# Eight experts streamed through one core: visiting them in an order worked out on chip

## The chip, the cores and the metric

The kernel runs on one core of a Trainium2 chip. The metric is the device time of one execution in microseconds (us). Before the change the median of three runs is 1410.58 us.

## The reference

Two decoder layers on 256 tokens of width 1024. Layer 0 has a convolution group beside an attention over a memory, then a dense SwiGLU. Layer 1 has a sliding-window attention beside the same memory attention, then the part that the change is about, eight experts of which each token uses two:

```
def moe_swiglu(h, router, we_gate, we_up, we_down):
    logits = (h @ router).astype(jnp.float32)
    top_v, top_i = lax.top_k(logits, TOP_K)
    top_w = jax.nn.softmax(top_v, axis=-1)
    gates = jnp.sum(jax.nn.one_hot(top_i, N_EXPERTS) * top_w[..., None], axis=-2)
    out = jnp.zeros_like(h)
    for e in range(N_EXPERTS):
        out = out + gates[..., e:e + 1] * swiglu(h, we_gate[e], we_up[e], we_down[e])
    return out
```

`swiglu(h, g, u, d)` is `(silu(h @ g) * (h @ u)) @ d`, with `g` and `u` 1024 x 3584 and `d` 3584 x 1024 for each expert, all float32. The sum over the experts may be taken in any order.

## The kernel before

After the two attention layers and the dense SwiGLU, the router's scores are worked out on chip, and for each token and expert its place among that expert's tokens (`posm`, L768) and its weight (`G`). With 256 tokens, two experts each and eight experts, an expert has 64 tokens on average. The kernel gives each expert a block of the first 64 tokens and a block of up to 32 more (`SL = 96`, L841); the second block is computed only if the expert has more than 64 tokens (`over`, L788). An expert with tokens past its 64th is called **long** here, one without **short**. (Tokens past the 96th would be done by a separate tail at the end; its branch is not taken here.)

**Rounds.** An expert's hidden width of 3584 is cut into four rounds of 896 (`rounds`, L681): 32 rounds, experts 0 to 7 in order. In a round, `gate_up` (L862) multiplies the gathered tokens `xe` with eight pieces of gate and up weights into the PSUM tiles `pa` and `pb` (L868). In the middle of it stand the transposes of the round before (`hidden_T`, L898) and, in some rounds, the scatter of a finished expert (L940) or the gather of the next one's tokens (L843). Then `over_parts` (L949) loads one flag into a register of TensorE's queue, and under `tc.If` (L956) does `gate_up_over` (L876, into `po`) for a long expert, and `down_over` (L927) for the round before, if that was of a long one. Last comes `down` (L917), which multiplies the hidden values of the round before with four pieces of down weights into `py`. The order on TensorE is written out by hand (L959); the other engines' order is the scheduler's.

**The weight stream.** Each round reads eight pieces of 896 KB (gate and up by turns) and four of the down matrix (three of 1024 KB, one of 512 KB). All are issued by SyncE's queue (SP) in the order of `units()` (L687 to L705): gate and up of round i, then down of round i-1. They go into a ring of 19 buffers of 1 MB (`RING`, L39): the piece number n waits until TensorE is done with the piece n-19. A gate or up piece is held until the round's `over_parts` is past, since both blocks read it. SP works in order, so a piece whose buffer is held also holds up all pieces behind it. `fetch` (L707, L991) writes the issues into the program a round at a time.

In the code after the change the same places stand some 50 to 60 lines further down.

Of the kernel before, what the change touches and what calls it, by code (L numbers as in the profile page):

```python
# [7 lines left out]
F32 = mybir.dt.float32  # L8
# [3 lines left out]
U32 = mybir.dt.uint32  # L12
AF = mybir.ActivationFunctionType
OP = mybir.AluOpType
AX = mybir.AxisListType
PSUM = bass.MemoryType.PSUM

P = 128
# [6 lines left out]
HD = 64  # L25
FF = 2816
NE = 8
# [20 lines left out]
def hybrid_kernel(  # L48
# [6 lines left out]
    nc = tc.nc  # L55
    act, dve, pool, pe, sp = nc.scalar, nc.vector, nc.gpsimd, nc.tensor, nc.sync
# [47 lines left out]
    for t in range(2):  # L104
# [5 lines left out]
                       channel_multiplier=1)  # L110
# [56 lines left out]
    with ExitStack() as ph:  # L167
# [377 lines left out]
        for i in range(NB):  # L545
# [15 lines left out]
            if prev is not None:  # L561
# [15 lines left out]
                           channel_multiplier=1)  # L577
        pool.affine_select(dist, dist, pattern=[[1, S]], compare_op=OP.is_ge, fill=BIG, base=-1,
                           channel_multiplier=-1)
# [11 lines left out]
        for blk in (2, 1, 0):  # L591
            w = [halves(load_rows(sw_w_in[0][i * 512:(i + 1) * 512, blk * 512:(blk + 1) * 512], 4),
                        after=last if blk == 1 else None) for i in range(2)]
# [29 lines left out]
        for n in range(2):  # L623
            for kp in range(2):
                b = bank("so", "so").rearrange("p (q n) -> p q n", n=P)
# [35 lines left out]
    with ExitStack() as ph:  # L661
        one = ph.enter_context(tc.tile_pool(name="one", bufs=1, reuse_waits="tile"))
# [14 lines left out]
        RW = 896  # L677
# [5 lines left out]
        def unit(v, src):  # L683
            sp.dma_start(v, src.rearrange("(k p) n -> p k n", p=P))  # L684
            return v

        def units():  # L687

            for i in range(len(rounds) + 1):
                if i < len(rounds):  # L690
                    e, p = rounds[i]
                    for q in range(4):
                        for w in (sw_we_gate, sw_we_up):
                            t = raw_tile()[:, :2 * RW].rearrange("p (k n) -> p k n", k=2)
                            yield unit(t, w[0, e, q * 256:(q + 1) * 256, p * RW:(p + 1) * RW])
                if i:
                    e, p = rounds[i - 1]
                    for q in range(4):
                        n = min(2, BLK - 2 * q)
                        t = raw_tile()[:, :n * D].rearrange("p (k n) -> p k n", k=n)  # L700
                        r0 = p * RW + 2 * q * P
                        yield unit(t, sw_we_down[0, e, r0:r0 + n * P, :])

        stream = units()
        ahead = []  # L705

# [10 lines left out]
        iota = one.tile([P, P], F32, name="iota")  # L717
        pool.iota(iota, pattern=[[1, P]], base=0, channel_multiplier=0, allow_small_or_imprecise_dtypes=True)

        rows2 = [one.tile([P, P], F32, name=f"rows2{n}") for n in range(2)]  # L720
        for n in range(2):
            o = (0, HD)[n]
            pool.tensor_copy(rows2[n][:, o:o + HD], iota[:, 0:HD])
            for q in range(2):
                pool.tensor_copy(rows2[n][:, HD - o + 32 * q:HD - o + 32 * q + 32], iota[:, HD:HD + 32])
        tri = one.tile([P, P], BF16, name="tri")
        pool.memset(tri, 1.0)
        pool.affine_select(tri, tri, pattern=[[1, P]], compare_op=OP.is_ge, fill=0.0, base=-1,
                           channel_multiplier=-1)
# [14 lines left out]
        for kk in range(KD // 2):  # L744
            b = prt.tile([P, 512], F32, name="rtb", tag="gu").rearrange("p (a n) -> p a n", a=2)
# [5 lines left out]
            for k in range(2 * kk, 2 * kk + 2):  # L751
                q = k % 4
# [15 lines left out]
        posm = one.tile([P, 2, NE], F32, name="posm")  # L768
# [12 lines left out]
        pn = bank("pn")  # L781
        for t in range(2):
# [3 lines left out]
                                 op0=OP.add, op1=OP.mult)  # L786
        dve.tensor_scalar_add(posm, posm, -1.0)
        over = one.tile([P, NE], I32, name="over")  # L788
        topi = one.tile([P, 1], I32, name="topi")
        G = one.tile([P, 2, NE], F32, name="G")  # L790
        dve.tensor_scalar(over, pn[:, :NE], float(HD), None, op0=OP.is_gt)
        top = one.tile([P, 1], F32, name="top")
        dve.reduce_max(top, pn[:, :NE], axis=AX.X)
        dve.tensor_copy(topi, top)
# [20 lines left out]
        def gates():  # L815

            gts = one.tile([P, 2, 2], F32, name="gts")
            dif = one.tile([P, 2, 1], F32, name="dif")
            eul = one.tile([P, 2], F32, name="eul")
            pool.memset(eul, 2.718281828459045)  # L820
            dve.tensor_tensor(dif, mx[:, :, 1:2], mx[:, :, 0:1], op=OP.subtract)
            ex = one.tile([P, 2], F32, name="ex")
            pool.tensor_tensor(ex, eul, dif[:, :, 0], op=OP.pow)
            den = one.tile([P, 2], F32, name="gden")
            dve.tensor_scalar_add(den, ex, 1.0)
            dve.reciprocal(gts[:, :, 0], den)
            dve.tensor_tensor(gts[:, :, 1], ex, gts[:, :, 0], op=OP.mult)
            for t in range(2):
                dve.tensor_scalar_mul(G[:, t, :], oh[:, t, 0, :], gts[:, t, 0:1])
                dve.scalar_tensor_tensor(G[:, t, :], oh[:, t, 1, :], gts[:, t, 1:2], G[:, t, :],  # L830
                                         op0=OP.mult, op1=OP.add)

        def places(e):

            Pm = [wk.tile([P, 2, P], F32, name=f"Pm{n}", tag=f"Pm{n}", bufs=1) for n in range(2)]
            for n in range(2):
                for t in range(2):
                    dve.tensor_scalar(Pm[n][:, t, :], rows2[n], posm[:, t, e:e + 1], None, op0=OP.is_equal)
            return Pm

        SL = 96  # L841
# [1 line left out]
        def gather(e, Pm):  # L843

            xe = wk.tile([P, KD, SL], F32, name="xe", tag="xe")
            for kk in range(2):
                b = bank("ga")[:, :4 * SL].rearrange("p (k n) -> p k n", k=4)
                for a in range(4):
                    k = kk * 4 + a
                    for t in range(2):  # L850
                        pe.matmul(b[:, a, :], hn[:, t, k * P:(k + 1) * P], Pm[0][:, t, :SL], start=(t == 0),
                                  stop=(t == 1))
                (act.copy if kk else dve.tensor_copy)(xe[:, kk * 4:kk * 4 + 4, :], b)
            b = bank("pmt")
            for n in range(2):
                for t in range(2):
                    pe.transpose(b[:, n * S + t * P:n * S + (t + 1) * P], Pm[n][:, t, :], ident)
            PT = wk.tile([P, 2, S], F32R, name="PT", tag="PT")
            act.copy(PT, b.rearrange("p (n s) -> p n s", n=2))
            return xe, PT  # L860
# [79 lines left out]
        def scatter(e, ys, PT):  # L940
            for n in range(2):
                for t in range(2):
                    b = bank("sc")
                    for i in range(2):
                        pe.matmul(b, PT[:, n, t * P:(t + 1) * P], ys[n][i], start=(i == 0), stop=(i == 1))
                    hs = h[:, t, n * 512:(n + 1) * 512]
                    dve.scalar_tensor_tensor(hs, b, G[:, t, e:e + 1], hs, op0=OP.mult, op1=OP.add)  # L947

        def over_parts(gu, dn):  # L949

# [7 lines left out]

        with tc.manual_schedule(engines={mybir.EngineType.PE}):  # L959
            xe = {0: gather(0, places(0))}  # L960
            gates()
            prev = None
            ys = None
            flag = None
            for i in range(len(rounds) + 1):
                last_round = i == len(rounds)
                if not last_round:
                    e, p = rounds[i]
                    wgu = [ahead.pop(0) for _ in range(8)]
                    if p == NR - 1 and e + 1 < NE:  # L970
                        Pm = places(e + 1)
                    gate_up(xe[e][0], wgu, range(4))
                if prev is not None:
                    wd = [ahead.pop(0) for _ in range(4)]
                    hT, hTo = hidden_T(*prev[2:])
                if ys is not None:
                    scatter(*ys)
                    ys = None
                if not last_round:
                    if p == NR - 1 and e + 1 < NE:  # L980
                        xe[e + 1] = gather(e + 1, Pm)
                    gate_up(xe[e][0], wgu, range(4, KD))
                    hx = hidden()
                over_parts(None if last_round else (e, p, xe[e][0], wgu), None if prev is None else (*prev[:2], hTo, wd))
                if prev is not None:
                    down(prev[1], hT, wd)
                    if prev[1] == NR - 1:
                        ys = (prev[0], outputs(), xe[prev[0]][1])
                if not last_round:
                    prev = (e, p, hx, hidden_over())  # L990
                    fetch(8 + 4 * (i > 0))  # L991
            scatter(*ys)
        finish()
        psm.close()
# [6 lines left out]
        def bank(name):  # L1001
# [6 lines left out]
                             skip_runtime_bounds_check_because="a count of 256 tokens")  # L1008
# [90 lines left out]
```

## Time and profile before

| | |
|---|---|
| median of 3 runs | 1410.58 us (1407.84 to 1410.89) |
| the profiled execution's own time | 1408.38 us |
| its span, first to last instruction | 1406.3 us |
| TensorE (PE) busy | 1290.9 us, 92% |
| VectorE (DVE) busy | 372.1 us, 26% |
| ScalarE (ACT) busy | 299.9 us, 21% |
| SP's DMA queue | 414.39 MB, 77.4% of 16 engines' span |
| mean granted clock of TensorE | 0.974 |

How to read it: a core's engines run side by side, each its own list of instructions in order, and wait for one another and for transfers. The shares are averages over the whole span; the experts' part is some 900 us of it, and has stretches with different limits. In the timelines PE is TensorE's matmul, an "x4" merges four like instructions, and square brackets give the idle time before an instruction and what ended it. "PEq" and "SPq" are the queues of TensorE and SyncE: instructions that load a register, branch or issue a transfer.

### The profile page before, as it was taken

What the parts mean: (1) busy time and instruction counts of PE and PEld (TensorE: products, weight loads), DVE (VectorE), ACT (ScalarE), POOL (GpSimd) and SP (SyncE); (2) the same over time, 40 slices, a digit from 0 to 9 for tenths busy, and PEclk for the clock granted to TensorE, in tenths of its full rate; (3) what the DMA queues carried; (4) which work ended last, traced back from release to release, by engine and by line L of the source; (5) the groups of instructions that cost most, each with busy time, mean ns of one, the idle gap of its engine ahead of it and who ended that gap; (6) DMA issues with size and microseconds to landing.
All of it is one profiled execution on the core that took longest, in us unless ns stands there. A gap on an engine that the chain in (4) does not pass through costs nothing. (4 is left out here: it accounts for less than half of the span.)

```text
span 1406.3 us, 18891 instructions
## 1 busy us (share of the span) xinstructions
PE 1290.9 (92%) x7908; PEld 711.0 (51%) x7908; DVE 372.1 (26%) x697; ACT 299.9 (21%) x575; POOL 70.2 (5%) x107
## 2 busy tenths in 40 slices
PE   6978899999889689999999999998888889999995
PEld 6844789999766533433344343443343343344342
DVE  5632554444676300102011111111111110100201
ACT  5423354444455010001001001111010010000100
POOL 5120100000030200000000000000000000000000
PEclk9989899999999899999999999999999999999998
DMA  9842155555470758899989989999999999999994
GB/s 294 290 120 57 61 197 190 183 180 180 111 244 1 288 198 312 316 361 367 377 335 378 360 334 361 405 406 406 407 406 407 407 407 406 407 407 406 404 407 189
DMA packets 149735, 420.90 MB, mean 299 GB/s; under 512 B 9658, under 2 KB 43256, under 8 KB 149624
## 3 DMA queue, kind: packets, MB, share of 16 engines
q1 hardware_dynamic: 145304, 414.39, 77.4%
q10 hardware_dynamic: 4320, 4.96, 1.1%
q8 instruction: 79, 1.29, 0.4%
q14 instruction: 32, 0.26, 0.1%
HBM read 417.37 MB, written 1.95 MB: 298 GB/s over the span
## 5 line engine op out<-in xcount | busy, mean ns | idle before, releaser
L868 PE MATMUL pa<-raw,xe 128*64 128x512 f32 x1024 | 302.9, 604 | 26.6 <-DMA raw<-in_sw_we_up_dram 19.1
L868 PE MATMUL pb<-raw,xe 128*64 128x384 f32 x1024 | 247.7, 493 | 0.0
L917 PE MATMUL py<-raw,hT 128*64 128x512 f32 x896 | 200.0, 596 | 17.2 <-PEq L956 16.0
L868 PEld LDWEIGHTS pb<-raw,xe 128*64 128x64 f32 x1024 | 87.8, 138 | 132.6 <-issue 128.7
L91 DVE TENSOR_TENSOR wlo<-raw,whi 128x1024 fp32r<-128x1024 f32 x108 | 131.9, 1260 | 81.7 <-ACT whi L90 81.7
L868 PEld LDWEIGHTS pa<-raw,xe 128*64 128x64 f32 x1024 | 83.3, 138 | 137.7 <-issue 86.7
L917 PEld LDWEIGHTS py<-raw,hT 128*64 128x64 f32 x896 | 66.6, 137 | 146.2 <-issue 114.0
L90 ACT CAST whi<-raw 128x1024 fp32r<-128x1024 f32 x112 | 111.5, 1046 | 55.5 <-issue 26.2
L876 PE MATMUL po<-raw,xe 128*32 128x512 f32 (+1 forms) x1024 | 113.1, 543 | 0.0
L910 DVE COPY hTo<-hto 128x224 f32<-128x224 f32 x32 | 12.5, 391 | 374.3 <-PE hto L908 374.3
L894 DVE TENSOR_TENSOR hxo<-so,po 64x384 f32<-64x384 f32 x32 | 17.8, 556 | 333.7 <-ACT so L893 333.7
L904 ACT COPY hT<-ht 128x448 f32<-128x448 f32 x32 | 17.0, 532 | 394.5 <-PE ht L902 394.5
L892 ACT ACTIVATE so<-po 64x384 f32<-64x384 f32 x32 | 15.4, 482 | 315.5 <-PE po L876 188.0
L876 PEld LDWEIGHTS po<-raw,xe 128*32 128x32 f32 x1024 | 39.6, 109 | 65.4 <-issue 59.2
L927 PE MATMUL py<-raw,hTo 128*32 128x512 f32 x448 | 65.5, 593 | 1.7 <-PEq L956 1.7
L98 PE MATMUL fg<-xh,whi 128*128 128x256 f32 x176 | 50.2, 285 | 2.7 <-ACT fsg L557 2.5
L98 PE MATMUL fu<-xh,whi 128*128 128x256 f32 x176 | 50.1, 284 | 0.0
L100 PE MATMUL fg<-xl,whi 128*128 128x256 f32 x176 | 50.0, 284 | 0.0
L99 PE MATMUL fu<-xh,wlo 128*128 128x256 f32 x176 | 50.0, 284 | 0.0
L99 PE MATMUL fg<-xh,wlo 128*128 128x256 f32 x176 | 50.0, 284 | 0.0
L100 PE MATMUL fu<-xl,whi 128*128 128x256 f32 x176 | 49.9, 284 | 0.0
L466 PE MATMUL pcv<-sh,bands 128*32 128x256 f32 x384 | 34.3, 425 | 12.1 <-DMA sh<-ud 12.0
(271 smaller groups left out, 1571.3 us busy)
## 6 DMA issues: line engine op xcount, KB each, us to landing
raw<-in_sw_we_gate_dram SPq DMA_DIRECT2D x128, 896.0 KB
raw<-in_sw_we_up_dram SPq DMA_DIRECT2D x128, 896.0 KB
raw<-in_sw_we_down_dram SPq DMA_DIRECT2D x96, 1024.0 KB
raw<-in_sw_we_down_dram SPq DMA_DIRECT2D x32, 512.0 KB
raw<-in_cv_w_gate_dram SPq DMA_DIRECT2D x11, 1024.0 KB
raw<-in_cv_w_up_dram SPq DMA_DIRECT2D x11, 1024.0 KB
raw<-in_cv_w_down_dram SPq DMA_DIRECT2D x11, 1024.0 KB
raw<-in_cv_w_in_dram SPq DMA_DIRECT2D x7, 1024.0 KB
```

What stands on the lines that cost most here:

```text
L90: act.copy(hi[:, i:i + step], v[:, i:i + step])
L91: (low or dve).tensor_tensor(lo[:, i:i + step], v[:, i:i + step], hi[:, i:i + step].bitcast(F32), op=OP.subtract)
L98: pe.matmul(ps, ah, bh, start=first, stop=False)
L99: pe.matmul(ps, al, bh, start=False, stop=False)
L100: pe.matmul(ps, ah, bl, start=False, stop=last)
L466: pe.matmul(pcv[q * 32:(q + 1) * 32, :], T[:, g, q, :], sh[q][:, 4 * g:4 * g + S], start=(g == 0), stop=(g == GT - 1), tile_position=(0, q ...
L868: pe.matmul(ps[half * HD:(half + 1) * HD, :c1 - c0], x, v[:, c0:c1], start=(k == 0), stop=(k == KD - 1), tile_position=(0, half * HD))
L876: pe.matmul(po[q * 32:(q + 1) * 32, :c1 - c0], x, v[:, k % 2, c0:c1], start=(k == 0), stop=(k == KD - 1), tile_position=(0, q * 32))
L894: dve.tensor_tensor(hx[:, :B], s[HD:, :B], po[HD:, :B], op=OP.mult)
L904: act.copy(hT, b[:, :3 * P + HD])
L917: pe.matmul(py[n][n * HD:(n + 1) * HD, :], hT[:, o:o + HD], w[q // 2][:, q % 2, n * 512:(n + 1) * 512], start=(p == 0 and q == 0), stop=(p ...
L927: pe.matmul(py[n][r:r + 32, :], hTo[:, o:o + 32], w[q // 2][:, q % 2, n * 512:(n + 1) * 512], start=(i < 2), stop=(i >= NR * BLK - 2), til ...
```

## The change

The experts are no longer taken in the order 0 to 7. Expert 0 stays first. For the others the order is worked out on VectorE from the eight counts: long and short ones by turns as far as both last, the first of them of the other kind than expert 0. The result is a row of eight indices `turn` and a 0/1 matrix `perm`, with which `posm`, `over` and `G` are put into the new order once (`posm2`, `over`, `G2`). The code of the rounds is then the same as before, with "expert e" meaning "the e-th in turn". The pieces of weights of all experts after the first are read from an address that depends on a register: SP loads `turn[e]` into a register once per expert, and each piece's address is that register times the size of one expert's matrix, plus a constant. Sizes, order and buffers of the pieces within an expert stay. The core of the diff:

```diff
+        turn = one.tile([P, NE], U32, name="turn")
+        whose = {0: 0}
+
+        def matrix(w, e):
+            if e not in whose:
+                whose[e] = nc.values_load(turn[0:1, e:e + 1], engines={mybir.EngineType.SP}, min_val=0, max_val=NE - 1,
+                                          skip_runtime_bounds_check_because="an index into eight numbers")
+            return w[0, 0] if e == 0 else w[0, bass.ds(whose[e], 1)][0]
...
-                            yield unit(t, w[0, e, q * 256:(q + 1) * 256, p * RW:(p + 1) * RW])
+                            yield unit(t, matrix(w, e)[q * 256:(q + 1) * 256, p * RW:(p + 1) * RW])
...
-                        yield unit(t, sw_we_down[0, e, r0:r0 + n * P, :])
+                        yield unit(t, matrix(sw_we_down, e)[r0:r0 + n * P, :])
...
+        before = one.tile([P, NE, NE], F32, name="before")
+        pool.memset(before, 1.0)
+        pool.affine_select(before, before, pattern=[[1, NE], [-1, NE]], compare_op=OP.is_ge, fill=0.0, base=-1,
+                           channel_multiplier=0)
+        pool.memset(before[:, :, 0:1], 0.0)
...
-        dve.tensor_scalar(over, pn[:, :NE], float(HD), None, op0=OP.is_gt)
+        dve.tensor_scalar(overf, pn[:, :NE], float(HD), None, op0=OP.is_gt)
...
+        def permuted(dst, src):
+            n = src.shape[1]
+            pr = one.tile([P, 2, NE, NE], F32, name="pr", tag="pr")
+            dve.tensor_tensor(pr[:, :n], perm[:, None].to_broadcast([P, n, NE, NE]),
+                              src[:, :, None, :].to_broadcast([P, n, NE, NE]), op=OP.mult)
+            dve.reduce_sum(dst, pr[:, :n], axis=AX.X)
+
+        def turns_of():
+            pr = one.tile([P, 2, NE, NE], F32, name="pr", tag="pr")[:, 0]
+            rk = one.tile([P, 4, NE], F32, name="rk")
+            val = one.tile([P, 8], F32, name="val")
+            turnf = one.tile([P, NE], F32, name="turnf")
+            dve.tensor_tensor(pr, before, overf[:, None, :].to_broadcast([P, NE, NE]), op=OP.mult)
+            dve.reduce_sum(rk[:, 0], pr, axis=AX.X)
+            dve.scalar_tensor_tensor(rk[:, 1], rk[:, 0], 2.0, iota[:, 0:NE], op0=OP.mult, op1=OP.subtract)
+            dve.scalar_tensor_tensor(rk[:, 2], rk[:, 1], 1.0, overf, op0=OP.add, op1=OP.mult)
+            dve.scalar_tensor_tensor(rk[:, 3], rk[:, 0], 1.0, iota[:, 0:NE], op0=OP.add, op1=OP.subtract)
+            dve.tensor_tensor(rk[:, 2], rk[:, 3], rk[:, 2], op=OP.subtract)
+            dve.tensor_scalar(rk[:, 1], overf, overf[:, 0:1], None, op0=OP.is_equal)
+            dve.scalar_tensor_tensor(val, rk[:, 2], 2.0, rk[:, 1], op0=OP.mult, op1=OP.subtract)
+            dve.memset(val[:, 0:1], 1.0)
+            best = one.tile([P, 8], F32, name="best")
+            dve.max(best, val)
+            dve.max_index(turn, best, val)
+            dve.tensor_copy(turnf, turn)
+            dve.tensor_tensor(perm, iota[:, None, 0:NE].to_broadcast([P, NE, NE]),
+                              turnf[:, :, None].to_broadcast([P, NE, NE]), op=OP.is_equal)
+            permuted(posm2, posm)
+            over2 = one.tile([P, 1, NE], F32, name="over2")
+            permuted(over2, overf[:, None, :])
+            dve.tensor_copy(over, over2[:, 0])
+
         def places(e):
+            pos = posm if e == 0 else posm2
...
-                    dve.tensor_scalar(Pm[n][:, t, :], rows2[n], posm[:, t, e:e + 1], None, op0=OP.is_equal)
+                    dve.tensor_scalar(Pm[n][:, t, :], rows2[n], pos[:, t, e:e + 1], None, op0=OP.is_equal)
...
-                    dve.scalar_tensor_tensor(hs, b, G[:, t, e:e + 1], hs, op0=OP.mult, op1=OP.add)
+                    dve.scalar_tensor_tensor(hs, b, G2[:, t, e:e + 1], hs, op0=OP.mult, op1=OP.add)
...
             xe = {0: gather(0, places(0))}
+            turns_of()
             gates()
+            permuted(G2, G)
```

On SP, at the place where the stream comes to the second expert (the last down pieces of the third round, then gate and up pieces of the fifth), there stood before:

```order
L684 DMA raw<-in_sw_we_down_dram 128x2x1024 x3
L684 DMA raw<-in_sw_we_down_dram 128x1024
L684 DMA raw<-in_sw_we_gate_dram 128x2x896
L684 DMA raw<-in_sw_we_up_dram 128x2x896
L684 DMA raw<-in_sw_we_gate_dram 128x2x896
```

and with the change, where ISA is an instruction that multiplies registers:

```order
L684 DMA raw<-in_sw_we_down_dram 128x2x1024 x3
L684 DMA raw<-in_sw_we_down_dram 128x1024
L693 TENSOR_LOAD turn
L684 ISA
L684 DMA raw<-in_sw_we_gate_dram 128x2x896
L684 ISA
L684 DMA raw<-in_sw_we_up_dram 128x2x896
L684 ISA
L684 DMA raw<-in_sw_we_gate_dram 128x2x896
```

One register load is added per expert after the first (7), and one ISA ahead of each of their pieces (7 x 48 = 336); no piece has moved in its queue.

On VectorE, at the start of the experts' part, between the gather matrix `Pm` of the first expert and the copy of its gathered tokens `xe`, there stood before:

```order
L838 TENSOR_SCALAR Pm_4455<-rows_4343,posm 128x128 x2
L827 TENSOR_TENSOR gts<-ex,gts 128x2
L829 TENSOR_SCALAR G<-oh,gts 128x8 x2
L830 SCALAR_TENSOR_TENSOR G<-oh,gts,G 128x8 x2
L853 COPY xe<-ga 128x384
```

and with the change:

```order
L895 TENSOR_SCALAR Pm_4464<-rows_4344,posm 128x128 x2
L869 TENSOR_REDUCE rk<-pr 128x8
...
L879 MAX best<-val 128x8
L880 MAX_INDEX turn<-best,val 128x8
L881 CAST turnf<-turn 128x8
L882 TENSOR_TENSOR perm<-iota,turnf 128x64
L858 TENSOR_TENSOR pr<-perm,posm 128x128
L860 TENSOR_REDUCE posm_4432<-pr 128x16
L910 COPY xe<-ga 128x384
L858 TENSOR_TENSOR pr<-perm,overf 128x64
```

Fourteen rows of the new ranking now stand ahead of that copy; one more (the product `pr` of `before` and `overf`, L868) stands ahead of `Pm`, and six behind the copy. On GpSimd (POOL) three rows that make `before` are added; on TensorE no instruction is added or moved.

## Rows read from the trace of the kernel before

**Rows 1.** DMA issues of the page: pieces of the weight stream, KB each.

```profile
raw<-in_sw_we_gate_dram SPq DMA_DIRECT2D x128, 896.0 KB
raw<-in_sw_we_up_dram SPq DMA_DIRECT2D x128, 896.0 KB
raw<-in_sw_we_down_dram SPq DMA_DIRECT2D x96, 1024.0 KB
raw<-in_sw_we_down_dram SPq DMA_DIRECT2D x32, 512.0 KB
```

**Rows 2.** Busy time by stretch: last three columns granted clock, DMA share, GB/s.

```profile
core 0: us, PE busy (x) PEld busy (x) DVE busy (x) ACT busy (x) POOL busy (x), PEclk, DMA share, GB/s
492.00:611.00 119.00, 115.29 (x747) 45.18 (x747) 11.49 (x28) 11.71 (x24) 0.00 (x0) 0.97 0.74 287
611.00:735.00 124.00, 124.00 (x814) 49.64 (x812) 15.01 (x31) 11.05 (x24) 0.00 (x0) 1.00 0.91 356
735.00:859.00 124.00, 124.00 (x814) 49.65 (x812) 15.01 (x31) 11.06 (x24) 0.00 (x0) 1.00 0.91 357
859.00:883.00 24.00, 23.11 (x130) 8.29 (x128) 2.39 (x5) 2.24 (x5) 0.00 (x0) 1.00 0.99 376
883.00:972.00 89.00, 84.42 (x446) 36.97 (x442) 15.02 (x31) 11.14 (x25) 0.00 (x0) 1.00 1.03 407
972.00:1083.00 111.00, 94.46 (x446) 41.76 (x446) 15.99 (x33) 12.05 (x26) 0.00 (x0) 0.98 1.03 407
1083.00:1197.00 114.00, 99.84 (x508) 44.11 (x509) 14.03 (x30) 9.98 (x22) 0.00 (x0) 0.99 1.03 407
1197.00:1316.00 119.00, 118.17 (x752) 47.14 (x750) 14.14 (x27) 11.06 (x24) 0.00 (x0) 1.00 1.03 406
```

**Rows 3.** The line of `gate_up_over`: in which of 40 slices it ran.

```profile
L876 PE MATMUL po<-raw,xe x1024: 486/552/617, 504.8 to 1282.0; 128*32 128x512 f32 x118, 128*32 128x384 f32 x53
busy tenths in 40 slices 0000000000000099999999999000000009999000
```

**Rows 4.** Timeline of TensorE: first matmuls of experts, `down_over` of expert 2, first missing piece.

```profile
611.25 1.03 PE L868 MATMUL pa<-raw,xe 128*64 128x512 f32 x4
735.20 1.03 PE L868 MATMUL pa<-raw,xe 128*64 128x512 f32 x4
859.13 1.03 PE L868 MATMUL pa<-raw,xe 128*64 128x512 f32 x4
873.42 3.63 PE L927 MATMUL py<-raw,hTo 128*32 128x512 f32 x28 [0.90 <-PEq L956]
951.03 1.06 PE L868 MATMUL pa<-raw,xe 128*64 128x512 f32 x4
972.52 1.04 PE L868 MATMUL pa<-raw,xe 128*64 128x512 f32 x2 [0.60 <-DMA raw<-in_sw_we_gate_dram]
1291.99 1.03 PE L868 MATMUL pa<-raw,xe 128*64 128x512 f32 x4
```

**Rows 5.** Waits of SP: which instruction waited for what, us in total, times, longest.

```profile
SPq L684 <- PE po L876: 253.2, 54, 32.5
```

**Rows 6.** Chain that ended last, two pieces: from a transfer's issue to its landing.

```profile
1351.67 16.97 DMA raw<-in_sw_we_gate_dram
1368.70 18.64 DMA raw<-in_sw_we_down_dram
```

**Rows 7.** Queue instructions: SP's issues, and register loads and branches of TensorE's queue.

```profile
459.58 0.37 SPq L684 DMA_DIRECT2D raw<-in_sw_we_up_dram  x1
460.04 0.42 SPq L684 DMA_DIRECT2D raw<-in_sw_we_gate_dram  x1
L954 PEldq TENSOR_LOAD <-over x64: 296/302/495, 501.1 to 1380.0; - x64
L956 PEldq COMPARE_BRANCH  x96: 65/169/431, 501.7 to 1380.4; - x96
```

**Rows 8.** Timeline of VectorE and TensorE at the start of the experts.

```profile
483.30 0.26 DVE L774 TENSOR_TENSOR oh<-iota,ixf 128x16 f32<-128x16 f32 x2
487.15 0.36 DVE L830 SCALAR_TENSOR_TENSOR G<-oh,gts,G 128x8 f32<-128x8 f32 x2
490.25 0.56 DVE L853 COPY xe<-ga 128x384 f32<-128x384 f32 x1 [2.74 <-PE ga L851]
492.64 1.08 PE L868 MATMUL pa<-raw,xe 128*64 128x512 f32 x4
```

More of the change, by code (lines that the diff above doesn't have):

```diff
@@ L788, in hybrid_kernel @@
         over = one.tile([P, NE], I32, name="over")
+        posm2 = one.tile([P, 2, NE], F32, name="posm2")
+        G2 = one.tile([P, 2, NE], F32, name="G2")
         topi = one.tile([P, 1], I32, name="topi")
         G = one.tile([P, 2, NE], F32, name="G")
-        dve.tensor_scalar(over, pn[:, :NE], float(HD), None, op0=OP.is_gt)
+        overf = one.tile([P, NE], F32, name="overf")
+        dve.tensor_scalar(overf, pn[:, :NE], float(HD), None, op0=OP.is_gt)
         top = one.tile([P, 1], F32, name="top")
@@ L831, in gates @@
                                          op0=OP.mult, op1=OP.add)
+        perm = one.tile([P, NE, NE], F32, name="perm")
+        def permuted(dst, src):
[28 more added lines that the diff above has]
+            dve.tensor_copy(over, over2[:, 0])
         def places(e):
+            pos = posm if e == 0 else posm2
             Pm = [wk.tile([P, 2, P], F32, name=f"Pm{n}", tag=f"Pm{n}", bufs=1) for n in range(2)]
```

## The prediction

> **What bounds the kernel now.** I read the stretches first, then TensorE's timeline, then the waits of SP and the chain that ended last.
>
> The weight stream is 128 + 128 pieces of 896 KB, 96 of 1024 KB and 32 of 512 KB [rows 1]: 352.3 MB, 44.04 MB an expert, 11.01 MB a round, and 0.918 MB a piece on average. The stretches [rows 2] show two regimes. From 883 us to 1316 us the transfers move 406 to 407 GB/s with little change, whatever TensorE does beside them: that is this stream's ceiling here, and at 407 GB/s an expert takes 108.2 us, a round 27.05 us and a piece 2.25 us. From 611 to 859 us they move only 356 and 357 GB/s, while TensorE is busy for all of the 248 us: there TensorE is the bound. Which experts these are is seen in the slices of the second block's matmuls [rows 3]: it runs in slices 14 to 24 and again in 33 to 36 (35.2 us each), so experts 0, 1, 2 and 6 are long, and 3, 4, 5 and 7 short.
>
> The timeline [rows 4] gives both prices on TensorE. A long expert after a long one takes 735.20 to 859.13, 123.9 us. The short one after it takes 859.13 to 951.03, 91.9 us, in which it still does the `down_over` of expert 2's last round, 3.63 us. So a long expert after a short one should take 123.9 - 3.6 = 120.3 us. The stream, at 108.2 us, lies between the two kinds: during a long expert it runs ahead until the ring is full, and then has to wait; during a short one TensorE eats up the lead.
>
> How large the lead can be shows after 859 us, where the ring is full. The four short rounds to 951.03 use up 108.2 - 91.9 = 16.3 us of it; the next round lasts to 972.52, 21.5 us against the stream's 27.05, 5.6 us more, and there TensorE waits for a piece for the first time [rows 4]. So a full ring is worth about **21.9 us** of lead.
>
> Three long experts in a row therefore cost what the ring cannot hold. SP waits 253 us in all for the second block to give buffers back, up to 32.5 us at a time [rows 5]. Afterwards three short ones in a row leave TensorE waiting for the stream. Both engines lose time, one after the other. The chain that ended last goes through two transfers of the stream near its end [rows 6]: the time of the whole is the stream's, plus what the stream lost before.
>
> **The change part by part.**
>
> *The order.* With these counts, the rank formulas give 0, 3, 1, 4, 2, 5, 6, 7: long and short by turns, a long one first and short expert 7 last, as before. The first long expert (to 611.25) and the change-over to a short one lose what they lose now. I then follow the lead from a full ring, 21.9 us: after expert 3, 5.6; expert 1 puts back 120.3 - 108.2 = 12.1, so 17.7; after 4, 1.4; after 2, 13.5; after 5, nothing, TensorE having waited 2.8; after 6, 12.1; at the end nothing, after another wait of 4.2. The lead never reaches 21.9 again, so the stream does not stop any more. What it loses now in experts 1 and 2 is saved: 124 x (1 - 356/407) + 124 x (1 - 357/407) = 15.5 + 15.2 = **30.8 us**. The 24 x (1 - 376/407) = 1.8 us of the change-over [rows 2] stay, as there is still one out of a full ring. That a long expert can run beside an unbroken stream is seen already: expert 6, after three short ones, has 406 GB/s from 1197 to 1316 us.
>
> *Whether TensorE is then the bound.* Its own path would be 611.25 + 3 x (91.9 + 120.3) = 1247.9 to the start of expert 7, and from there to the end of the span it takes 1406.3 - 1291.99 = 114.3 us today: 1362 us. The stream's end gives 1406.3 - 30.8 = 1375.5. The stream decides, by 13 us; this also limits a gain to 44 us.
>
> *Addresses from registers.* SP gets 336 register multiplications and 7 register loads. Before, no such multiplication is in the trace. The nearest rows [rows 7] are a branch on a register, 0.17 us, and a register load on TensorE's queue, 0.30 us; an issue takes 0.37 us and the next one comes 0.46 us later. With 0.30 us more each, twelve pieces of a round need 12 x 0.76 = 9.1 us of SP's 27. The last transfers on the chain take 17 and 18.6 us from issue to landing [rows 6], which is seven or eight pieces: SP is that far ahead, and a register load of 0.3 us, or a late multiplication, lies under this cover. I take nothing for it, between nothing (it can't speed up SP) and the price in the last rival. If a piece's address were needed while the ring is full, its buffer would be the later one anyway. SP reads `turn` only after three rounds of issues, long after VectorE made it; what stands behind that load are the pieces of the second expert, not needed for two more rounds.
>
> *The ranking.* One product is new ahead of `Pm` and so on TensorE's path: 0.13 to 0.26 us by its neighbours [rows 8], I take 0.2. Fourteen rows (15 instructions in a trace, since an index search shows as two) stand ahead of the copy of `xe`. At 0.18 to 0.26 us each [rows 8] they take 2.7 to 3.9 us. VectorE idles 2.74 us there, and the copy, which ends at 490.81, is wanted only when TensorE is through with its transposes at 492.64: 1.8 us more. The cover is 4.6 us, so nothing is lost; without it the sum would grow by up to 3.9 us. `over` is read 9 us later [rows 7], the second expert's `Pm` in the fourth round. GpSimd's three rows are on no chain.
>
> *The sum.* The profiled execution took 1408.38 us with a span of 1406.3, so 2.1 lie outside. 1408.4 - 30.8 + 0.2 = 1377.8 us. The median of the runs is 2.2 us above that execution: **1380.0 us**.
>
> **A rule that speaks against it.** The trace has the stream at 407 GB/s for over 400 us [rows 2]. The Trainium skill, DMA: Bandwidth & Descriptors, section Bandwidth, puts one core's share of its memory at about 358 GB/s and says that "For HBM↔SBUF transfers the HBM side (~358) binds". By that rule the 356 and 357 GB/s of experts 1 and 2 would already be the ceiling and nothing could be saved: 1410.6 us instead of 1380.0. The trace goes against it here; this core reads alone.
>
> **The rivals.**
>
> 1. *The ring fills up in other ways.* What stops SP may be less the lead than the bunching of a long round, in which all eight gate and up buffers come back within the second block. For it: SP's 253 us of waits for just that [rows 5]. Against it: expert 6, the same rounds with a low lead, loses nothing [rows 2]. If each of the three later long experts lost a third of the 15.4 us of now, the gain would be halved: 1395 us.
> 2. *No change.* Either 357 GB/s is a ceiling of that stretch, or the order on chip comes out as the old one. Against the first stands 407, against the second the counts behind rows 3. Time: 1410.6 us.
> 3. *Slower: SP's issue takes the stream's place as the bound.* Once an address comes from a register, an issue could cost more than a piece takes to move. It decides from 2.25 - 0.46 = 1.8 us extra per piece; beyond this, 336 pieces pay the excess, so the gain is gone at 30.8/336 = 0.09 us more, about 1.9 us. At 2.0 us extra the sum is 336 x 0.21 - 30.8, some 40 us slower: 1450 us. For it: nothing in this trace, only that no register-addressed transfer is in it. Against it: the queue instructions that are, at 0.17 and 0.30 us [rows 7].
>
> **How the numbers follow.** Forecast 0.82; rival 1, 0.08; rival 2, 0.05; rival 3, 0.05. The forecast's own range is 1374 to 1386 us: the runs spread over 3 us, a ceiling of 406 or 409 GB/s for the 765 us left moves it by 2 to 4, and VectorE's 3.9 us could come uncovered. To hold 8 in 10 I widen it towards rival 1, to 1373 to 1391. A measurement of this kernel can tell about 0.2%, 3 us, from no change: faster 0.90 (forecast and rival 1), same 0.05, slower 0.05.
>
> **What would show it.** In the new profile: the second block in four stretches with gaps between them; 406 GB/s or so in every slice from the second expert to the end; a last DMA wait of TensorE at most a few us long; SP's waits for `po` down to those of the first expert and a few short ones. Rates under 390 GB/s in later long experts would say rival 1, SP issues over 1.8 us with the transfers idle rival 3.

## The result, and the profile after

| | before | changed |
|---|---|---|
| median of 4 runs each | 1410.74 us (1407.84 to 1412.88) | 1378.41 us (1373.13 to 1380.02) |
| the profiled execution's own time | 1408.38 us | 1378.21 us |
| its span | 1406.3 us | 1376.4 us |
| experts' part, first `gate_up` matmul to the end of the span | 913.7 us | 884.4 us |

The ratio is 0.9766, with a 95% interval of 0.9734 to 0.9797: faster, and 1.6 us beside the 1380.0 us that were forecast. The profiled execution gains 29.9 us. 29.3 of them lie in the experts' part and 0.6 ahead of it, which is itself a gain of 3.3 and a loss of 2.7; the last section takes these apart.

From the page of the changed kernel: the GB/s of the 40 slices (34.4 us each, counted from 0). Below them stands the line of the second block's matmuls.

```profile
GB/s 288 286 131 74 62 134 202 188 185 185 119 221 81 212 184 289 375 336 393 406 406 406 406 407 406 406 407 407 406 406 406 407 406 407 407 406 404 402 407 168
```

```profile
L933 PE MATMUL po<-raw,xe x1024: 486/552/617, 504.2 to 1250.0; 128*32 128x512 f32 x118, 128*32 128x384 f32 x53
busy tenths in 40 slices 0000000000000099990099990009990009999000
```

The second block runs in four stretches with gaps between them, where it ran in two [rows 3]: long and short experts come by turns. No row names the experts; that the order is 0, 3, 1, 4, 2, 5, 6, 7 follows from the formulas and from which experts were long before. From slice 19 (653 us) to slice 38 the stream is never below 402 GB/s.

The stretches of the changed kernel, one an expert as far as the last (columns as in [rows 2]):

```profile
492.00:611.00 119.00, 115.29 (x743) 44.83 (x744) 11.41 (x28) 11.47 (x24) 0.00 (x0) 0.97 0.74 290
610.00:702.00 92.00, 87.94 (x474) 37.31 (x472) 15.01 (x31) 11.07 (x24) 0.00 (x0) 1.00 1.02 401
702.00:824.00 122.00, 121.64 (x788) 49.41 (x786) 15.01 (x31) 11.06 (x24) 0.00 (x0) 1.00 1.03 407
824.00:916.00 92.00, 87.83 (x474) 37.74 (x471) 15.01 (x31) 11.06 (x24) 0.00 (x0) 1.00 1.03 406
916.00:1042.00 126.00, 123.72 (x786) 50.76 (x785) 15.01 (x31) 11.06 (x24) 0.00 (x0) 1.00 1.03 407
1042.00:1134.00 92.00, 87.88 (x474) 37.31 (x471) 15.02 (x31) 11.07 (x24) 0.00 (x0) 1.00 1.03 406
1134.00:1260.00 126.00, 123.69 (x786) 50.52 (x785) 14.14 (x27) 11.06 (x24) 0.00 (x0) 1.00 1.03 406
```

No long expert after the first has 356 or 357 GB/s any more. The second one (702 to 824 us) is the one to look at: TensorE is busy for all of it, as it was in experts 1 and 2 before, and the stream has 407 GB/s all the same.

TensorE's timeline, the first matmuls of four experts and four waits for a piece:

```profile
610.62 1.03 PE L925 MATMUL pa<-raw,xe 128*64 128x512 f32 x4
702.43 1.06 PE L925 MATMUL pa<-raw,xe 128*64 128x512 f32 x4
824.25 1.03 PE L925 MATMUL pa<-raw,xe 128*64 128x512 f32 x4
...
921.64 0.64 PE L925 MATMUL pa<-raw,xe 128*64 128x512 f32 x1 [1.22 <-DMA raw<-in_sw_we_up_dram]
930.61 0.64 PE L925 MATMUL pa<-raw,xe 128*64 128x512 f32 x1 [0.70 <-DMA raw<-in_sw_we_up_dram]
1139.35 0.64 PE L925 MATMUL pa<-raw,xe 128*64 128x512 f32 x1 [1.14 <-DMA raw<-in_sw_we_up_dram]
1148.44 0.64 PE L925 MATMUL pa<-raw,xe 128*64 128x512 f32 x1 [0.81 <-DMA raw<-in_sw_we_up_dram]
1260.06 1.03 PE L925 MATMUL pa<-raw,xe 128*64 128x512 f32 x4
```

The short expert takes 702.43 - 610.62 = 91.8 us and the long one behind it 121.8. After 824 us TensorE begins to run out of pieces: its waits for the stream are the four of the timeline, in the first rounds of the third and the fourth long expert, and two in the last expert (0.76 and 0.56 us). One more, of 0.90 us at 838.54 in expert 4, is put down to a transfer; but the three other short experts wait 0.83 to 0.90 us for the branch at the same place, so it is hardly the stream's. The third and the fourth long expert take 126.0 us each. Ahead of them the forecast had the lead at 1.4 us and at nothing.

What SP waited for. First the whole span, then the stretch from 492 to 620 us:

```profile
SPq L684 <- PE po L933: 141.1, 44, 32.1
```

```profile
SPq L684 <- PE po L933: 92.7, 15, 32.1
```

253.2 us have become 141.1 [rows 5], and 92.7 of these are in the first expert, which had 93.9 before. Behind it 159.3 have become 48.4, and these don't show in the GB/s. The longest of them is 5.5 us, while a piece near the end is 17 to 19 us on its way: SP holds while transfers that it issued before are still landing.

Registers, on SP's timeline in the fifth round:

```profile
650.23 0.37 SPq L684 DMA_DIRECT2D raw<-in_sw_we_up_dram  x1
650.84 2.19 SPq L684 DMA_DIRECT2D raw<-in_sw_we_down_dram  x4
653.27 0.37 SPq L684 DMA_DIRECT2D raw<-in_sw_we_gate_dram  x1
653.89 2.02 SPq L684 DMA_DIRECT2D raw<-in_sw_we_up_dram  x1
```

From one issue to the next it is 650.84 - 650.23 = 0.61 us, where it was 0.46 [rows 7]: 0.15 to 0.16 us for the multiplication of registers.

The ranking, on VectorE's timeline between the gather matrix and the copy of the gathered tokens:

```profile
485.57 0.74 DVE L895 TENSOR_SCALAR Pm<-rows,posm 128x128 f32<-128x128 f32 x4
486.23 0.21 DVE L869 TENSOR_REDUCE rk<-pr 128x8 f32<-128x64 f32 x1
...
489.25 0.29 DVE L860 TENSOR_REDUCE posm<-pr 128x16 f32<-128x128 f32 x1
489.67 0.56 DVE L910 COPY xe<-ga 128x384 f32<-128x384 f32 x1
```

The fifteen instructions end at 489.54, just ahead of the copy. Behind the copy stand five of the added rows (six were counted above). From `Pm` to the copy it is 4.10 us in both kernels (486.15 to 490.25 before, 485.57 to 489.67 after).

### The profile page after: what moved, and what is told of

Same layout as the page of the kernel before. It is cut to its first block, busy times and chain, and to the rows that moved or that the text cites. A ratio compares the mean times of both kernels' runs of the same rounds, so it can differ in the third digit from the quotient of the medians.

```text
span 1376.4 us, 19594 instructions
## 1 busy us (share of the span) xinstructions
PE 1280.9 (93%) x7908; PEld 704.9 (51%) x7908; DVE 375.6 (27%) x718; ACT 300.0 (22%) x575; POOL 70.6 (5%) x110
## 3 DMA queue, kind: packets, MB, share of 16 engines
q8 instruction: 79, 1.29, 0.4%
HBM read 417.37 MB, written 1.95 MB: 305 GB/s over the span
## 5 line engine op out<-in xcount | busy, mean ns | idle before, releaser
L925 PE MATMUL pa<-raw,xe 128*64 128x512 f32 x1024 | 281.3, 600 | 8.3 <-DMA raw<-in_sw_we_up_dram 4.6
L925 PE MATMUL pb<-raw,xe 128*64 128x384 f32 x1024 | 225.2, 489 | 0.0
L925 PEld LDWEIGHTS pb<-raw,xe 128*64 128x64 f32 x1024 | 81.9, 138 | 138.6 <-issue 136.8
L925 PEld LDWEIGHTS pa<-raw,xe 128*64 128x64 f32 x1024 | 78.1, 137 | 105.3 <-issue 75.6
L90 ACT CAST whi<-raw 128x1024 fp32r<-128x1024 f32 x112 | 111.6, 1048 | 55.1 <-issue 26.2
L949 ACT ACTIVATE so<-po 64x384 f32<-64x384 f32 x32 | 15.4, 482 | 311.8 <-PE po L933 161.9
```

What stands on the lines that cost most here:

```text
L90: act.copy(hi[:, i:i + step], v[:, i:i + step])
L925: pe.matmul(ps[half * HD:(half + 1) * HD, :c1 - c0], x, v[:, c0:c1], start=(k == 0), stop=(k == KD - 1), tile_position=(0, half * HD))
```

## The experiments

The theory is that of the prediction: with long and short experts by turns the ring's lead goes up and down without filling, so the stream does not stop; registers and ranking lie under cover. Against it stood the ring filling in other ways (rival 1), a price on SP (rival 3), and, once the profile was there, something outside the experts' part. Every ratio below is to the kernel before, run on the same chip.

**1. The order alone, written in; the parts on chip alone.** The first kernel is the one before with a fixed order, which stands in the addresses and the columns of `posm`, `over` and `G`:

```diff
+        ORDER = (0, 3, 1, 4, 2, 5, 6, 7)
...
-                            yield unit(t, w[0, e, q * 256:(q + 1) * 256, p * RW:(p + 1) * RW])
+                            yield unit(t, w[0, ORDER[e], q * 256:(q + 1) * 256, p * RW:(p + 1) * RW])
...
```

> The order 0, 3, 1, 4, 2, 5, 6, 7 written into the program: no ranking on chip, fixed addresses, otherwise the kernel before. If the order alone makes the gain and ranking and register addresses cost nothing: 1378 us, a ratio of 0.977 to the kernel before, like the changed kernel within 3 us. If they do cost something that the gain hid: faster than the changed kernel by that, 1375 us or less. If the gain came from something else in the change: 1410 us.

The second keeps everything of the change, but its ranking gives the old order:

```diff
-            dve.scalar_tensor_tensor(val, rk[:, 2], 2.0, rk[:, 1], op0=OP.mult, op1=OP.subtract)
+            dve.scalar_tensor_tensor(val, rk[:, 2], 0.0, iota[:, 0:NE], op0=OP.mult, op1=OP.subtract)
```

> The changed kernel with a factor of 0 in the ranking, so that it gives 0 to 7: all its instructions, register loads and register addresses, but the old order. If the order alone makes the gain: 1411 us, within 3 us of the kernel before. If register addresses cost time wherever the ring is what SP waits for (in experts 0 to 2): slower than before, 336 x 0.1 us or more, 1415 us and up. If the addresses or the ranking made the gain: 1378 us.

Measured: the fixed order 1381.14 us, ratio 0.9801 (0.9782 to 0.9820), experts' part 883.5 us; the old order on chip 1406.58 us, ratio 0.9976 (0.9964 to 0.9987), experts' part 914.0 us. So the order gives the 29 to 30 us of the experts' part, and registers with ranking cost under 1 us there (914.0 against 913.7, 884.4 against 883.5). Left over were 3 us in the runs: the kernel with everything but the order was not equal to the one before but 3.2 us faster by the medians.

**2. Other orders.** Three more tables in the kernel of the fixed order. Four long ones first, 0, 1, 2, 6, 3, 4, 5, 7:

> Order 0, 1, 2, 6, 3, 4, 5, 7 written in: the four long experts first. Theory (a long expert that meets a full ring costs the stream 15.4 us): three such behind the first instead of two, so 15 us slower than before, 1426 us. Rival (what matters is only that short ones lie between): no different from before, 1411 us.

Pairs, 0, 1, 3, 4, 2, 6, 5, 7:

> Order 0, 1, 3, 4, 2, 6, 5, 7 written in: two long, two short, two long, two short. By the lead alone (a full ring is worth 21.9 us): expert 1 loses 15.4; two short ones use up all; 2 and 6 put back 12.1 and 15.7, 27.8 in all, so 6 us too much for the ring; loss 21 us instead of 30.8, so 1401 us. By the bunching of buffers within a long round (the ring is full well before the lead is): a long expert behind a long one always loses some 15 us, so 2 x 15, 1409 to 1411 us.

And short ones first by turns, 3, 0, 4, 1, 5, 2, 7, 6:

> Order 3, 0, 4, 1, 5, 2, 7, 6 written in (no shift of memory): by turns as well, but a short one first and a long one last. The first expert then takes the lead of a full ring at once, so the stream loses some 15 us less in the first 119 us than in alt_fixed; the last expert is a long one that TensorE works off after the stream has ended, 12 us longer than a short one in the stream's time, and its last round has the second block and down_over besides. If both ends weigh the same: within 4 us of alt_fixed's 1381. If only the stream's losses count: 1366 us.

Four long ones first: 1424.17 us, ratio 1.0097 (1.0069 to 1.0125). Its stretches of the three later long experts:

```profile
611.00:735.00 124.00, 124.00 (x814) 49.65 (x812) 15.02 (x31) 11.06 (x24) 0.00 (x0) 1.00 0.92 354
735.00:859.00 124.00, 124.00 (x814) 49.65 (x812) 15.02 (x31) 11.06 (x24) 0.00 (x0) 1.00 0.91 358
859.00:986.00 127.00, 127.00 (x828) 50.65 (x826) 15.01 (x31) 11.06 (x24) 0.00 (x0) 1.00 0.91 354
```

Each long expert behind a full ring loses 15 to 17 us; the third one's loss makes the experts' part 929.1 us, 15.4 more than before. The same expert 6 that had 406 GB/s behind short ones [rows 2] has 354 here, so it is the place in the order and not the expert.

Pairs: 1404.48 us, ratio 0.9968 (0.9950 to 0.9986), experts' part 909.4 us. Its second pair:

```profile
932.00:1059.00 127.00, 124.74 (x792) 50.96 (x790) 15.02 (x31) 11.06 (x24) 0.00 (x0) 1.00 1.03 406
1059.00:1183.00 124.00, 124.00 (x816) 49.70 (x814) 15.01 (x31) 11.06 (x24) 0.00 (x0) 1.00 0.94 367
```

This came out between the theories. The first of the pair loses nothing, the second 124 x (1 - 367/407) = 12.2 us, twice the 6 us that were expected by the lead alone. The expectation counted the lead from nothing at the start of the pair. The timeline shows that TensorE is out of pieces only inside the first round, last at its eighth piece:

```profile
947.33 0.64 PE L869 MATMUL pa<-raw,xe 128*64 128x512 f32 x1 [0.73 <-DMA raw<-in_sw_we_up_dram]
1182.90 1.03 PE L869 MATMUL pa<-raw,xe 128*64 128x512 f32 x4
```

From that wait to the end of the pair it is 235.6 us. In them TensorE uses the round's four down pieces and seven more rounds, 9.0 + 7 x 27.05 = 198.4 us of the stream's time. 235.6 - 12.2 - 198.4 leaves a lead of 25.0 us. The prediction's own stretch gives nearly the same for a full ring, once the 1.8 us that the stream lost in it are counted: 21.9 + 1.8 = 23.7. So pairs does not show a ring that fills before its lead is reached; the lead starts from nothing inside a round, and not at the round's start. In the changed kernel the same count from 1148.44 to 1260.06 us gives 111.6 - 9.0 - 3 x 27.05 = 21.4 us, which still fits, by some 2 us.

Short ones first: 1378.84 us, ratio 0.9786 (0.9764 to 0.9808), the same as the change. The page's GB/s show how:

```profile
GB/s 303 278 142 54 62 162 204 185 185 184 93 221 81 230 179 386 407 407 406 406 407 407 406 407 407 407 406 406 407 406 406 407 399 404 406 407 406 406 316 35
```

The start loses less (386 GB/s in slice 15, where the changed kernel has 289), but the last expert is then a long one, worked off when the stream is through: 316 and 35 GB/s in the last two slices, against 407 and 168. By these rates slices 15 to 18 win 34.4 x 213/407 = 18.0 us, and the last two give back 34.4 x 224/407 = 18.9. What is won at one end is paid at the other.

**3. A smaller ring.** The changed kernel with 15 buffers for 19:

```diff
-RING = ("xn", "xh", "xl", "raw", "raw") + ("raw",) * 4 + ("xh", "xl") + ("whi", "wlo") * 4
+RING = ("xn", "raw", "raw") + ("raw",) * 4 + ("whi", "wlo") * 4
```

> The changed kernel with four of the 19 buffers left out of the ring. By the lead alone a full ring is then worth 21.9 - 4 x 2.25 = 12.9 us, a long expert puts back 12.1 and so still fits: 1378 us, but for a microsecond or two at the start. If the ring holds the stream up well before that lead is reached (in pairs the experts 2 and 6 together lost 12 us where the lead alone gave 6): each later long expert loses again, 1390 to 1410 us, and most of the gain is gone.

Measured: 1396.75 us, ratio 0.9908 (0.9880 to 0.9937): some 18 of the 32 us are gone. GB/s of its slices (34.9 us each):

```profile
GB/s 288 280 137 62 61 163 199 182 182 182 106 223 8 227 176 304 363 334 407 407 406 407 406 364 393 406 407 407 407 370 390 407 406 406 407 407 359 392 407 223
```

There are three dips, 364 and 393, 370 and 390, 359 and 392, each at the end of a long expert and the start of the short one behind it. 34.9 x (43 + 14)/407 = 4.9 us for the first, and likewise 4.6 and 5.4: 14.9 us in all. The expectation's first half was wrong, and by the same count as in pairs. In this kernel too TensorE waits for a piece in the first round of each later long expert, the last time at its eighth piece, and then works to the expert's end in 111.6 us:

```profile
721.42 0.64 PE L925 MATMUL pa<-raw,xe 128*64 128x512 f32 x1 [0.72 <-DMA raw<-in_sw_we_up_dram]
833.05 1.03 PE L925 MATMUL pa<-raw,xe 128*64 128x512 f32 x4
```

So each of them would put back 21.4 us, and not 12.1, into a ring that is worth 23.7 - 9.0 = 14.7 with four pieces less: a loss of some 7 us each is due by the lead alone, and three dips of nearly one size follow, as each starts from an empty ring. They are smaller than that, 4.6 to 5.4. That the ring fills in another way, as rival 1 has it, is not needed for any of these losses, though no run that gives the gate and up pieces back earlier excludes it.

**4. A price put on SP.** In the changed kernel each address of the experts after the first gets extra register loads whose values cancel, two or eight:

```diff
...
+            v = whose[e]
+            for i in range(8):
+                r = nc.values_load(turn[0:1, e:e + 1], engines={mybir.EngineType.SP}, min_val=0, max_val=NE - 1,
+                                   skip_runtime_bounds_check_because="an index into eight numbers")
+                v = v - r if i % 2 else v + r
...
-            return w[0, 0] if e == 0 else w[0, bass.ds(whose[e], 1)][0]
+            return w[0, bass.ds(v, 1)][0]
```

> The changed kernel; each piece's address takes two more register loads on SP (they cancel in the sum), 0.6 us at the 0.30 us of such a load on TensorE's queue, with 0.62 us from one issue to the next without them: 1.2 us, still under the 2.25 us that a piece takes to move. If SP's time per issue lies under the stream: no difference, 1378 us. If it is on the path even in part: 336 x 0.6 x that part, so 1400 us at a tenth and more.

> The same with eight register loads: 8 x 0.30 + 0.62 = 3.0 us per piece, over the 2.25 us that it takes to move. If an issue decides only beyond a piece's transfer: SP becomes the bound, 336 x (3.0 - 2.25) = 260 us slower than the changed kernel, 1640 us, with TensorE waiting for transfers in every round and the transfers idle between pieces. If the price of a load is under 0.2 us on SP, 1378 us.

With two: 1377.01 us, ratio 0.9772 (0.9743 to 0.9800), the time of the change. SP's timeline has the issues 1.29 us apart:

```profile
659.19 0.37 SPq L684 DMA_DIRECT2D raw<-in_sw_we_up_dram  x1
660.48 0.37 SPq L684 DMA_DIRECT2D raw<-in_sw_we_gate_dram  x1
```

With eight: 1733.88 us, ratio 1.2305 (1.2269 to 1.2341). The issues are 3.36 us apart, and the stretch has no more than 271 GB/s:

```profile
730.41 0.37 SPq L684 DMA_DIRECT2D raw<-in_sw_we_up_dram  x1
733.77 0.37 SPq L684 DMA_DIRECT2D raw<-in_sw_we_gate_dram  x1
```

```profile
740.00:1700.00 960.00, 763.69 (x3700) 300.11 (x3698) 87.45 (x177) 65.18 (x142) 0.00 (x0) 0.93 0.82 271
```

A load with its addition costs (3.36 - 0.62)/8 = 0.343 us, more than the 0.30 that was put in, so the time is above the 1640 us expected. With the measured spacing the sum holds: 336 x (3.36 - 2.25) = 373 us, less the 21.9 of a full ring's lead at the start, is 351, and 1733.88 - 1378.41 is 355. So there is an edge between 1.29 and 3.36 us, as rival 3 had it at 2.25, and the change, at 0.62, is far below it.

**5. The 3 us ahead of the experts.** The first experiment left a gain that the order does not explain. From the last `xt` transposes of layer 1's first norm (L213) to the first `gate_up` matmul it was 115.2 us before (377.4 to 492.64) and 111.9 after (380.1 to 492.04). What lies there and differs is the load of the norm's `gain` on SP. Before:

```profile
460.04 0.42 SPq L684 DMA_DIRECT2D raw<-in_sw_we_gate_dram  x1
463.80 0.35 SPq L674 DMA_DIRECT2D gain<-in_sw_ffn_norm_g_dram  x1
```

Changed:

```profile
462.72 0.42 SPq L684 DMA_DIRECT2D raw<-in_sw_we_gate_dram  x1
463.24 0.42 SPq L674 DMA_DIRECT2D gain<-in_sw_ffn_norm_g_dram  x1
```

Before, 3.76 us pass between the two issues, and the waits of SP name TensorE and an attention tile as the cause; after, it is 0.52 us. The row of before:

```profile
SPq L674 <- PE so L285: 3.3, 1, 3.3
```
The diff does not touch this load, but it adds tiles of some 1.5 KB to the pool `one`, and the tiles made later then lie elsewhere in memory. To test that, the kernel before got one tile that nothing reads, ahead of `gain`:

```diff
+        pad = one.tile([P, 368], F32, name="pad")
+        pool.memset(pad[:, 0:1], 0.0)
```

> The kernel before with 1472 bytes per partition of an unused tile ahead of the tile gain, so that gain lies where it does in the changed kernel; order and fixed addresses as before. If the 0.24% of reg_old_order come from gain's load, which before waits for an attention tile on whose memory it lies: the load goes out right behind the piece ahead of it, the experts start 3 us earlier, ratio 0.9975, some 1406.5 us. If they come from the register addresses or the ranking: no difference, 1409.8 us.

Measured: 1408.07 us, ratio 0.9989 (0.9976 to 1.0002): smaller than the expected 0.9975, and not clear of no change. The runs alone do not settle it. The profile does: the load follows the piece before at once, and 111.9 us lie between the two marks (378.1 to 489.96).

```profile
460.67 0.42 SPq L686 DMA_DIRECT2D raw<-in_sw_we_gate_dram  x1
461.19 0.42 SPq L676 DMA_DIRECT2D gain<-in_sw_ffn_norm_g_dram  x1
```

All twelve profiles agree: from the marks of `xt` to the experts it is 115.0 to 115.2 us in the five kernels in which the load of `gain` waits (before, and the four with a fixed order and no pad), and 111.9 to 112.1 in the seven in which it does not.

The last run joins both, the fixed order and the pad:

> alt_fixed with the unused tile of pad_only: the alternating order written in, fixed addresses, no ranking, and gain's load free of the wait for the attention tile. If the changed kernel's gain is the order plus this shift of memory and nothing else: the experts start 112 us after the last transposes of layer 1's first norm, as in the changed kernel (115 in alt_fixed), and the runs agree with the changed kernel, 1378 us, 1 to 3 us below alt_fixed's 1381. If the shift is worth nothing: 1381 us.

Measured: 1378.65 us, ratio 0.9777 (0.9761 to 0.9793), 111.9 us ahead of the experts and 884.6 in them. The changed kernel has 1378.41, 111.9 and 884.4. Within the scatter of the runs, the order and a tile's place in memory make up the whole of the change.

No order here was clearly faster than the change. Loading `gain` early on purpose was not tried.

## Why the prediction was right

- **The saving.** 30.8 us were forecast from the 356 and 357 GB/s of experts 1 and 2; the experts' part gained 29.3 (the 0.2 for VectorE's product lie ahead of it). The six experts between the first and the last now take 1260.06 - 610.62 = 649.4 us, six times the 108.2 of the stream, where they took 1291.99 - 611.25 = 680.7 [rows 4]: 31.3 us less. The last expert takes 2.0 us more than before (116.3 for 114.3), 1.2 of them up to the landing of the last piece; what does that is open. Fixed order and long ones first show the saving with both signs, the latter at 15.4 us for one long expert more behind a full ring.
- **The change-over** from the first long expert was to cost 1.8 us: 92 x (1 - 401/407) = 1.4.
- **The lead** is the weak step, right in its result with some luck. Forecast were 1.4 us left ahead of the third long expert, a wait of 2.8 in the short one ahead of the fourth, and one of 4.2 in the last expert. Measured were 1.92 us in the first round of the third long expert, 1.95 in that of the fourth, by the idle times of the four rows, and 1.3 in the last expert. The reason is that TensorE uses a long round's eight gate and up pieces, 18.0 us of the stream, in some 13 us (from 702.43 to the second block at 715.78), so that a lead of some 5 us at the round's start is used up inside it. Counted from there, the later peaks are not 13.5 and 12.1 us but 21.4, under a full ring of 23.7: 2 us to spare, where the forecast saw 8 and more. A long expert after a short one took 121.8 us where 120.3 was worked out; 0.36 of the 1.5 us are a wait for the branch (723.21 us), the rest lies in no wait that the trace names.
- **TensorE as the next bound** was put at 1362 us. That its waits for pieces come back says that the stream, not TensorE, still sets the end; the chain that ended last passes through three transfers of it. The last of them, from its issue to its landing:

```profile
1338.02 18.57 DMA raw<-in_sw_we_down_dram
```

- **Registers.** Nothing was taken for them, between nothing and rival 3. An address costs 0.16 us of SP, the time did not move when issues stood 1.29 us apart, and the edge lies beyond that.
- **The ranking.** The cover of 4.6 us held for the 15 instructions, which end 0.13 us ahead of the copy; the copy came no later. The product ahead of `Pm` lengthened its way by 0.14 us (0.2 forecast).
- **The ceiling.** The Trainium skill, DMA: Bandwidth & Descriptors, section Bandwidth, has about 358 GB/s as the binding share of a core. The same section of the Trainium skill has each core at about that rate when both cores of a memory domain stream. The long expert at 702 to 824 us had 407, and the 356 of before turned into it by the order alone; the measurement decides, and one core reads here.
- **Not foreseen** is the 3.3 us of the `gain` load. It went into a median that has a scatter of the same size in it (last section), so the 1.6 us between forecast and median test no single term; the part-by-part numbers above do.

## What to carry to other kernels

Where stretches bound by the engine and stretches bound by the stream alternate in one queue, their order is worth time: a ring that stays neither full nor empty keeps the stream going, and the two durations with the stream's rate tell beforehand how far the lead swings. Count the lead piece by piece inside the rounds, from the place where the engine last waited; counted from expert to expert it came out 8 to 9 us too small here, and two expectations missed by it. Addresses from registers are free as long as an issue, with all that stands ahead of it, takes less than the piece it moves; and before a few us are credited to an edit, compare the parts of the span that it does not touch.

## What the runs showed that was not expected

**A tile that nothing reads can move time.** 1.5 KB in one pool changed where a later tile lies, took a 3.26 us wait off SP and started the experts 3.3 us earlier on the same marks:

```profile
L213 PE MATMUL xt<-ident,xn x48: 270/358/478, 8.2 to 377.4; 128*128 128x128 f32 x48
```

```profile
L213 PE MATMUL xt<-ident,xn x48: 270/415/478, 8.2 to 380.1; 128*128 128x128 f32 x48
```

These are the marks of before and after, and they show a second thing: the point itself falls anywhere from 375.1 us (the kernel with eight loads) to 381.5, in kernels that are alike up to there (377.7 for the fixed order, 380.7 for the same with the pad, 380.9 for the long ones first). I did not find what decides it; it is why a gain of 3 us is hard to see in medians and plain in the profile.

**A register load on SP's queue** took 0.267 us at the median in the kernel with eight of them, and 0.343 with its addition. **Issue to landing** of a piece near the end is 17 to 19 us in both kernels [rows 6], some eight pieces under way. That depth is the likely reason why SP could wait 48.4 us after the first expert, 5.5 us at a time at most, without a gap in the stream.
